# Streaming both parts of x past one loaded weight tile in a feed-forward up-projection

## The chip, the cores and the metric

The kernel runs on one core of a Trainium2 chip. The metric is device time in microseconds (us) of one execution of the whole program, the median of the runs shown. Engines are named as the profile names them: PE is the matrix engine (TensorE), PEld its weight loads, DVE the vector engine, ACT the scalar engine, POOL the GpSimd engine, SP the queue that issues the loads from memory.

## The reference

Two layers of a decoder on an input of 256 positions by 1024 features, in float32. Each layer is a mixer (three branches, merged and projected) and then a feed-forward block, each followed by a layer norm. The change touches only the feed-forward block:

```python
def _swiglu(x, w1, w3, w2):
    h = jax.nn.silu(jnp.einsum("bsd,df->bsf", x, w1)) * jnp.einsum("bsd,df->bsf", x, w3)
    return jnp.einsum("bsf,fd->bsd", h, w2).astype(x.dtype)
```

Here x is 256 x 1024, w1 and w3 are 1024 x 2816, w2 is 2816 x 1024. The two products with w1 and w3 are the up-projections; the one with w1 goes through silu and gates the other.

## The kernel before

**Numbers in two parts.** Matrix products run on numbers of type float32r, which keep fewer bits than float32. To keep accuracy, each float32 value is split into a high part (ACT copies it into float32r, `hi`) and a low part (DVE subtracts the high part from the value, `lo`). A product W x is then three products: W_hi x_hi + W_hi x_lo + W_lo x_hi. Each of the three is a matrix instruction of its own, with its own weight load, and all add into the same PSUM bank.

**The weights** stream from memory in units of 128 x 1024 floats (512 KB), one after the other in a fixed order, into four raw buffers. Each unit is split by one ACT and one DVE instruction (`split_w`, lines 416 to 438) into a `hi` and a `lo` tile. The split units are kept up to six ahead of PE (`AHEAD`, `fill`).

**The feed-forward block** of a layer has three stretches. The first 512 of the 2816 hidden columns are made token-major (tile `tm`, 512 columns of weights stream past x). The other 2304 hidden columns are made feature-major, 128 at a time: for f from 4 to 21, one unit of w1 and one of w3 (tile `f13`, shown as `f` in the profile). Then comes the down-projection with w2 (tile `w`), 22 units, into four banks (in the last layer five).

**One f in the kernel before** (lines 1274 to 1280): a PSUM bank of 512 columns is taken; w1's product fills its left 256 columns (the 256 positions), w3's its right 256. For each product `fm_acc` (line 458) runs over eight slices k of the 1024 features, three matrix instructions of 256 columns each. The side chain `f_fm` (line 1124) then reads the bank: ACT takes silu of the left half into `sg`, DVE multiplies the right half into `sg`, ACT and DVE split `sg` into the tiles `hh` (both parts are named so) that the down-projection uses.

**The order of the work.** All instructions of an engine run in the order in which they are emitted. That order comes from the class `Order` (line 159): it keeps an estimated clock for each engine, emits the main stream of matrix products, and emits the next step of a side chain once its estimate says that what the step needs is done. PSUM has eight banks, taken in turn; the small tiles such as `sg` have two buffers each.

**The parts of x** lie in four tiles of 1024 floats per partition (`xtile`, line 476), each with the high parts of two slices k in its first half and the low parts of the same two slices in its second.

Of the kernel before, what the change touches and what calls it, by code (L numbers as in the profile page):

```python
# [155 lines left out]


class Order:
    """Emission order: a main stream of matrix products and side chains whose next stage
    is emitted once the stage before it is expected to be done."""  # L160

    def __init__(self):
        self.clk = {e: 0.0 for e in ("pe", "act", "dve", "pool", "dma")}
# [86 lines left out]
def _build(ctx, nc, tc, ins, out):  # L250
# [87 lines left out]
    def rsqrt(o, i, e):  # L338
        G.tensor_tensor(out=o, in0=i, in1=e, op=ALU.pow)  # L339
        O.op("pool", 0.3 + 0.17 * n_of(o))  # L340
# [20 lines left out]
    def p2(t):  # L361
        return t.rearrange("p (t c) -> p t c", t=2)

    def pair2(name, dt=F32):
        return [p2(t) for t in pair(name, dt)]
# [4 lines left out]
    def rows(ap, n=P):  # L370
        return ap[:, None, :].to_broadcast([n, 4, P])

# [1 line left out]
    kc = const.tile([P, NK], F32, name="kc")  # L374
    xr = xres.tile([P, 2, D], F32, name="xr")
    ident = kc[:, K_ID:K_ID + P]
# [16 lines left out]
    sh8 = [P, 2, 4]  # L393
    mh8 = mhalf.rearrange("p (t h) -> p t h", t=2)

# [1 line left out]
    raws, ready, pos = [], [], [0, 0]  # L397

    def halves(i):
# [56 lines left out]
        return x[k // 2][:, k % 2]  # L456

    def fm_acc(o, w, x, c=slice(None)):
        """o[feature, token] = W^T x; w = (hi, lo) [128, k, columns], x = (hi, lo) tiles."""
        nk = w[0].shape[1]  # L460
        for k in range(nk):
            mm(o, w[0][:, k, c], xk(x[0], k), k == 0, False)
            mm(o, w[0][:, k, c], xk(x[1], k), False, False)
            mm(o, w[1][:, k, c], xk(x[0], k), False, k == nk - 1)

    def tm_acc(o, x, tk, w, k0, first, last):
        """o[token, column] += x^T W for the k-tiles of one unit from k-tile k0 on."""
        sl = slice(tk * P, (tk + 1) * P)
        nk = w[0].shape[1]
        for k in range(nk):  # L470
            xh, xl = (xk(x[q], k0 + k)[:, sl] for q in range(2))
            mm(o, xh, w[0][:, k], first and k == 0, False)
            mm(o, xl, w[0][:, k], False, False)
            mm(o, xh, w[1][:, k], False, last and k == nk - 1)

    def xtile(name):
        t = [pair2(name, F32R) for _ in range(4)]
        return [[a[q] for a in t] for q in range(2)]

    def log1p(o, t, tag, shape):  # L480
        """o = log(1 + t), t >= 0, compensated."""
        u, lg, e, d = (sm(tag + n, shape) for n in "uled")
        ts(u, t, 1.0, ADD)
        act_fn(lg, u, AF.Ln)
        ts(e, u, 1.0, ALU.is_equal)
        stt(d, u, -1.0, e, ADD, ADD)
        recip(d, d)
        tt(lg, lg, e, ADD)
        tt(lg, lg, t, MULT)
        tt(o, lg, d, MULT)  # L490

    def layer(l, xs, xtok):
# [5 lines left out]
        def done(n):  # L498
            O.done(k_(n))

# [1 line left out]
        def conv(dst, ps, w, ct, nct, bias):  # L502
            wv = lambda k, t: vc(w + nct * k + ct + t)
            for t in range(2):
# [51 lines left out]
            return  # L556
            yield

# [1 line left out]
        def b_scal():  # L560
            yield k_("smf")
            smf = B["smf"]
# [78 lines left out]
        def b_inv():  # L641
# [30 lines left out]
            B["bk"] = bk  # L672
            done("bk")
            yield
            # inverses of the diagonal 8x8 blocks by forward substitution: partition =
            # column of the inverse, each block's rows spread over its partitions
            at8 = AT.rearrange("p (t c) -> p t c", t=8)
            c32 = sub[:, 0:256].rearrange("p (t c) -> p t c", t=8)
            ac, z, tmp = (sub[:, 256 + 64 * n:320 + 64 * n].rearrange("p (t c) -> p t c", t=8)
# [143 lines left out]
            done("vb")  # L823

        def norm_gate(os, rs, gate, name, wo):
            """y = o rs rsqrt(mean((o rs)^2) + eps) w gate, to feature-major parts."""
            ss, f, m = (sm(name + n, sh8) for n in ("s", "f", "m"))
            sq = pair4("sq")
            for tk in range(2):
                act_fn(sq[tk], os[tk], AF.Square)  # L830
            yield
            for tk in range(2):
                rowsum(ss[:, tk], sq[tk])
            if rs is not None:
                tt(m, rs, rs, MULT)
                tt(ss, m, ss, MULT)
            ts(m, ss, 1.0 / P, MULT, 1e-6, ADD)
            yield
            rsqrt(f, m, mh8)
            if rs is not None:  # L840
                tt(f, f, rs, MULT)
            yield
            ys = pair4(name + "y")
            for tk in range(2):
                y = ys[tk]
                for h in range(4):
                    stt(y[:, h], os[tk][:, h], f[:, tk, h:h + 1], h4(B[gate, tk])[:, h],
                        MULT, MULT)
            yield
            hi, lo = [], []  # L850
            for t in range(2):
                ps = bank("pyf").rearrange("p (t k c) -> p t k c", t=2, k=2)
                for q in range(2):
                    for tk in range(2):
                        tp(ps[:, q, tk], ys[tk][:, 2 * t + q], ident)
                ps = ps.rearrange("p t k c -> p t (k c)")
                a, b = pair2(name + "h", F32R)
                act_fn(a, ps, AF.Copy, scale=vc(wo))
                stt(b, ps, vc(wo), a.bitcast(F32), MULT, SUB)
                hi.append(a), lo.append(b)  # L860
            B[name] = (hi, lo)
            done(name)

# [1 line left out]
        def c_copy(ps, nm):  # L865
            if nm == "cq":
                B["cqk"] = pair2(nm)
# [61 lines left out]
                co.append(o)  # L929
            yield from norm_gate(co, None, "sr", "yc", V_CN)  # L930

# [1 line left out]
        def a_gate(ps, j):  # L933
            ps = p2(ps)
            if j == 0:
# [60 lines left out]
            B["ya"] = yh, yl  # L996
            done("ya")

# [1 line left out]
        def g_chain(ps, b, j):  # L1000
            ps = p2(ps)
            if j % 2 == 0:
# [97 lines left out]
                r.append(t)  # L1100
            return r

# [1 line left out]
        hh = [None] * (NF // 2)  # L1104
        hl = [None] * (NF // 2)

# [5 lines left out]
        def f_tm(p3, tk):  # L1112
# [8 lines left out]
                split(*(x[:, :, tk * P:(tk + 1) * P] for x in h_tiles(q)), ps[:, 2 * q:2 * q + 2])  # L1121
            done(f"hT{tk}")

        def f_fm(ps, f):
            ps = p2(ps)
            sg = sml.tile([P, S], F32, tag="sg", name="sg")
            act_fn(sg, ps[:, 0], AF.Silu)
            yield
            tt(sg, ps[:, 1], sg, MULT)
            yield  # L1130
            hi, lo = h_tiles(f // 2)
            split(hi[:, f % 2], lo[:, f % 2], sg)
            done(f"h{f}")

# [1 line left out]
        def tm_group(x, chains, second):  # L1136
            """512-column token-major projections of four units each; with `second` the
            first token tile goes first, and the second once that token is there."""
            if second is None:
                for chain in chains:  # L1140
                    ps = [bank("tm") for _ in range(2)]
                    for q in range(4):
                        w = unit(2)
                        for tk in range(2):
                            tm_acc(ps[tk], x, tk, w, 2 * q, q == 0, q == 3)
                        if q == 3:
                            for tk in range(2):
                                O.spawn(chain(ps[tk], tk), 1)
                        yield
                return  # L1150
            u = []
            for tk in range(2):
                if tk:
                    yield second
                for n, chain in enumerate(chains):
                    ps = bank("tm")
                    for q in range(4):
                        if tk == 0:
                            u.append(unit(2, 1))
                        else:  # L1160
                            held[0] -= 1
                        tm_acc(ps, x, tk, u[4 * n + q], 2 * q, q == 0, q == 3)
                        if q == 3:
                            O.spawn(chain(ps, tk), 1)
                        if tk:
                            fill()
                        if q % 2:
                            yield
# [9 lines left out]
        def main():  # L1178
# [12 lines left out]
            O.spawn(small(pss), 0)  # L1191
            O.spawn(b_scal(), 2)
            yield
            mh, ml = xtile("mh")
            seen = []
            for u in MIX:
                nm, i = u[:-1], int(u[-1])
# [33 lines left out]
                    O.spawn(b_q(), 2)  # L1231
                if u == "v1":
                    O.spawn(b_v(), 2)
            # output projection
            if l == 0:
                nc.sync.dma_start(out=xr, in_=ins["xtm"])
            lv = ln_vecs(0)
# [19 lines left out]
            for tk in range(2):  # L1257
                for i in range(8 - tail, 8):
# [7 lines left out]
                    if i == 7:  # L1266
                        ahead[0] = 0
                    yield
            # feed-forward: hidden columns 0..511 token-major, the rest feature-major
            yield k_("x10")  # L1270

            yield from tm_group(x1, [lambda ps, tk: silu_tm(ps, "s1", tk), f_tm], k_("x11"))
            lv = ln_vecs(1)
            for f in range(4, NF):
                ps = bank("f13")
                for q in range(2):
                    fm_acc(p2(ps)[:, q], unit(8), x1)
                    if q:
                        O.spawn(f_fm(ps, f), 1)
                    yield  # L1280
            last = l + 1 == L
            x2 = None if last else xtile("x2")
# [40 lines left out]

        return main(), B, (k_("x20"), k_("x21"))

# [1 line left out]
    def everything():  # L1327
        xs, tok = xs0, ("xin", "xin")
        for l in range(L):
# [2 lines left out]
            xs, tok = B["x2"], t2_  # L1332

    with tc.manual_schedule(engines={mybir.EngineType.SP}):
        # the array's clock rises to its full rate only after some busy microseconds: let
        # it run while the first loads are under way
        warm = sml.tile([P, 512], BF16, tag="warm", name="warm")
        V.memset(warm, 0.0)
        pw = bank("warm")
# [108 lines left out]
```

## Time and profile before

| | us |
|---|---|
| median of 3 runs | 947.45 |
| lowest, highest | 945.55, 948.33 |
| span of the profiled execution | 945.9 |
| PE busy | 928.2 |
| DVE busy | 618.4 |
| ACT busy | 503.2 |

The profiled execution's own time is not given beside its span; the span runs from its first instruction to its last. Matrix instructions are pipelined: the duration shown for one reaches from its start to the modelled end of its passage, and overlaps the next one. How fast PE goes through a stream of them is therefore read from the distance between their starts, or from the length of a stretch and the number of instructions in it.

### The profile page before, as it was taken

What the parts mean: (1) busy time and instruction counts of PE and PEld (TensorE: products, weight loads), DVE (VectorE), ACT (ScalarE), POOL (GpSimd) and SP (SyncE); (2) the same over time, 40 slices, a digit from 0 to 9 for tenths busy, and PEclk for the clock granted to TensorE, in tenths of its full rate; (3) what the DMA queues carried; (4) which work ended last, traced back from release to release, by engine and by line L of the source; (5) the groups of instructions that cost most, each with busy time, mean ns of one, the idle gap of its engine ahead of it and who ended that gap; (6) DMA issues with size and microseconds to landing.
All of it is one profiled execution on the core that took longest, in us unless ns stands there. A gap on an engine that the chain in (4) does not pass through costs nothing.

```text
span 945.9 us, 16798 instructions
## 1 busy us (share of the span) xinstructions
PE 928.2 (98%) x6882; PEld 869.8 (92%) x6882; DVE 618.4 (65%) x893; ACT 503.2 (53%) x752; POOL 164.0 (17%) x81
## 2 busy tenths in 40 slices
PE   8999899999999999999999999999999999999996
PEld 5999799999988999998889999999999889999885
DVE  5587975595875655566457699586758646555715
ACT  5777569634633554455145775974547145444510
POOL 0445512630000000000033251254200000000001
PEclk9999999999999999999999999999999999999999
DMA  8854324546770855578325343254668247555801
GB/s 281 254 177 144 107 67 130 173 151 228 257 278 19 283 189 181 187 238 289 108 86 200 102 149 112 71 171 162 201 217 277 107 142 259 178 179 178 287 25 45
DMA packets 47997, 162.92 MB, mean 172 GB/s; under 512 B 7536, under 2 KB 8496, under 8 KB 47792
## 3 DMA queue, kind: packets, MB, share of 16 engines
q1 hardware_dynamic: 47776, 161.71, 51.2%
q8 instruction: 54, 0.88, 0.4%
q14 instruction: 23, 0.19, 0.1%
q10 hardware_dynamic: 144, 0.13, 0.0%
HBM read 160.77 MB, written 1.05 MB: 171 GB/s over the span
## 4 chain that ended last, share of the span: by engine, by line
PE 81%; DVE 9%; ACT 3%; DMA 3%; issue 2%; POOL 1%; SPq 0%; POOLq 0%; ACTq 0%; DVEq 0%
PE f L347 22%; PE fm L347 21%; PE w L347 13%; PE tm L347 8%; PE br L347 7%; PE wo L347 4%; DMA raw<-in_w_dram 3%; DVE lo L304 2%; ACT hi L292 1%; PE pt L347 1%; PE pp L347 1%; DVE sub L304 1%; DVE xa L315 1%; DVE q L315 1%; PE pr L347 1%
## 5 line engine op out<-in xcount | busy, mean ns | idle before, releaser
L304 DVE TENSOR_TENSOR lo<-raw,hi 128x1024 fp32r<-128x1024 f32 (+1 forms) x241 | 309.3, 1307 | 113.4 <-ACT hi L292 107.1
L292 ACT ACTIVATE hi<-raw 128x1024 fp32r<-128x1024 f32 (+1 forms) x293 | 299.3, 1052 | 92.3 <-DMA raw<-in_w_dram 83.0
L347 PE MATMUL fm<-x,hi 128*128 128x256 f32 x1536 | 283.7, 286 | 0.0
L347 PEld LDWEIGHTS fm<-x,hi 128*128 128x128 f32 x1536 | 240.0, 192 | 2.1 <-issue 1.5
L347 PE MATMUL fm<-x,lo 128*128 128x256 f32 x768 | 217.8, 284 | 0.0
L347 PE MATMUL f<-x,hi 128*128 128x256 f32 x1152 | 207.7, 283 | 0.0
L347 PEld LDWEIGHTS f<-x,hi 128*128 128x128 f32 x1152 | 179.8, 192 | 0.2
L432 POOL TENSOR_TENSOR lo<-raw,hi 128x1024 fp32r<-128x1024 f32 x52 | 136.0, 2617 | 231.0 <-ACT hi L292 227.4
L347 PE MATMUL f<-x,lo 128*128 128x256 f32 x576 | 163.0, 283 | 0.0
L347 PEld LDWEIGHTS fm<-x,lo 128*128 128x128 f32 x768 | 147.5, 192 | 0.0
L347 PE MATMUL w<-hi,hh 128*128 128x512 f32 (+1 forms) x396 | 111.2, 367 | 0.0
L347 PEld LDWEIGHTS f<-x,lo 128*128 128x128 f32 x576 | 110.6, 192 | 0.0
L347 PE MATMUL tm<-hi,x 128*128 128x512 f32 x320 | 100.8, 398 | 2.5 <-ACT hi L292 2.5
L339 POOL TENSOR_TENSOR rs<-rs,mhalf 128x1 f32<-128x1 f32 x8 | 7.5, 937 | 530.4 <-DVE rs L309 530.4
L347 PEld LDWEIGHTS w<-hi,hh 128*128 128x128 f32 x396 | 71.4, 189 | 12.2
L347 PEld LDWEIGHTS tm<-hi,x 128*128 128x128 f32 x320 | 59.2, 190 | 15.7 <-ACT hi L292 4.1
L347 PE MATMUL w<-lo,hh 128*128 128x512 f32 (+1 forms) x198 | 72.4, 365 | 0.0
L347 PE MATMUL tm<-lo,x 128*128 128x512 f32 x160 | 62.1, 391 | 0.1
L304 DVE TENSOR_TENSOR sg<-f,sg 128x256 f32<-128x256 f32 x36 | 15.1, 420 | 58.7 <-ACT sg L292 58.7
L292 ACT ACTIVATE sg<-f 128x256 f32<-128x256 f32 x36 | 13.8, 384 | 73.7 <-PE f L347 73.7
L347 PEld LDWEIGHTS w<-lo,hh 128*128 128x128 f32 x198 | 37.3, 188 | 6.1
L347 PE MATMUL wo<-hi,mh 128*128 128x512 f32 x128 | 40.0, 393 | 0.5 <-ACT mh L292 0.5
(273 smaller groups left out, 1092.0 us busy)
## 6 DMA issues: line engine op xcount, KB each, us to landing
raw<-in_w_dram SPq DMA_DIRECT2D x291, 512.0 KB, 4.6
lnv<-in_lnv_dram SPq DMA_DIRECT2D x8, 512.0 KB, 8.0
xr<-in_xtm_dram SPq DMA_DIRECT2D x1, 1024.0 KB, 8.3
xin<-in_xfm_dram SPq DMA_DIRECT2D x3, 256.0 KB, 7.3
raw<-in_w_dram SPq DMA_DIRECT2D x2, 256.0 KB, 3.5
ar<-in_aw_dram SPq DMA_DIRECT2D x8, 64.0 KB, 4.4
out_dram<-xr SPq DMA_DIRECT2D x2, 256.0 KB, 2.1
kc<-in_kc_dram SPq DMA_DIRECT2D x1, 476.0 KB, 8.8
```

Source lines behind the costliest of these rows:

```text
L292: ins_ = A.activation(o, i, f, **k)
L304: V.tensor_tensor(out=o, in0=a, in1=b, op=op)
L315: V.scalar_tensor_tensor(out=o, in0=a, scalar=s, in1=b, op0=op0, op1=op1)
L339: G.tensor_tensor(out=o, in0=i, in1=e, op=ALU.pow)
L347: T.matmul(o, w, x, start=start, stop=stop)
L432: G.tensor_tensor(out=lo, in0=t, in1=hi.bitcast(F32), op=SUB)
```

## The change

The eight slices of a unit take two matrix instructions each instead of three. The first streams 512 columns past the weight's high part: the 256 of x_hi and, from the other half of the same tile, the 256 of x_lo. They land in the left and the right half of one bank. The second streams x_hi past the weight's low part and adds to the left half. So a bank holds one unit's product only, in two halves that must be added when it is read: ACT copies the right half to SBUF, DVE adds the left half to it. w1's unit gets a side chain of its own (`f_gate`: copy, add, then silu), w3's another (`f_fm`: copy, add, multiply by the gate, split). `xtile` returns a third view of the same memory, in which the two parts of a slice stand beside each other. Only the feature-major up-projections of the feed-forward block change (18 f in each of two layers, two units each: 72 units); the mixer's feature-major projections still use `fm_acc`. Comments were removed too, and blank lines put in their place.

```diff
+    def fm_acc2(o, w, x):
+        nk = w[0].shape[1]
+        for k in range(nk):
+            mm(o, w[0][:, k], x[2][k // 2][:, k % 2], k == 0, False)
+            mm(o[:, 0], w[1][:, k], xk(x[0], k), False, k == nk - 1)
...
     def xtile(name):
-        t = [pair2(name, F32R) for _ in range(4)]
-        return [[a[q] for a in t] for q in range(2)]
+        v = [slot(name, F32R).rearrange("p (q k c) -> p k q c", q=2, k=2) for _ in range(4)]
+        return [t[:, :, 0] for t in v], [t[:, :, 1] for t in v], v
...
+        def f_gate(ps, f):
+            sg = sml.tile([P, S], F32, tag="sg", name="sg")
+            B["sg", f] = sg
+            cp(sg, ps[:, 1])
+            tt(sg, ps[:, 0], sg, ADD)
+            yield
+            act_fn(sg, sg, AF.Silu)
+            done(f"sg{f}")
+
         def f_fm(ps, f):
-            ps = p2(ps)
-            sg = sml.tile([P, S], F32, tag="sg", name="sg")
-            act_fn(sg, ps[:, 0], AF.Silu)
-            yield
-            tt(sg, ps[:, 1], sg, MULT)
+            sg = B["sg", f]
+            hv = sml.tile([P, S], F32, tag="hv", name="hv")
+            cp(hv, ps[:, 1])
+            tt(hv, ps[:, 0], hv, ADD)
+            yield k_(f"sg{f}")
+            tt(sg, hv, sg, MULT)
             yield
             hi, lo = h_tiles(f // 2)
             split(hi[:, f % 2], lo[:, f % 2], sg)
...
             for f in range(4, NF):
-                ps = bank("f13")
-                for q in range(2):
-                    fm_acc(p2(ps)[:, q], unit(8), x1)
-                    if q:
-                        O.spawn(f_fm(ps, f), 1)
+                for chain in (f_gate, f_fm):
+                    ps = p2(bank("f13"))
+                    fm_acc2(ps, unit(8), x1)
+                    O.spawn(chain(ps, f), 1)
                     yield
```

The order of the instructions on PE at the start of the feature-major stretch of the first layer (tile `f_3502` is the bank, `x_3157` the tile of x, `hi` and `lo` the parts of the weight unit; "x2" means two in a row; `-` is before, `+` after):

```order
 L347 MATMUL tm<-hi,x_3160 128x512 x2
 L347 MATMUL tm<-lo,x_3160 128x512
-L347 MATMUL f_3502<-x_3157,hi 128x256 x2
+L347 MATMUL f_3502<-x_3157,hi 128x512
 L347 MATMUL f_3502<-x_3157,lo 128x256
```

Two products of 256 columns with the same weight became one of 512; this repeats for every slice, and apart from it and from the bank that w3's unit writes, PE's order is the same in the whole program.

The order on ACT in the middle of that stretch, over two f, in the kernel before (`sg` is the gate, `hh` the split hidden column, `hi<-raw` the split of a weight unit):

```order
L292 ACTIVATE sg_4064<-f13_3966 128x256
L292 ACTIVATE hh_4000<-sg_4064 128x256
L292 ACTIVATE sg_4130<-f13_4033 128x256
L292 ACTIVATE hh_4133<-sg_4130 128x256
L292 ACTIVATE hi_4136<-raw_4007 128x1024
L292 ACTIVATE hi_4167<-raw_4038 128x1024
L292 ACTIVATE hi_4202<-raw_4073 128x1024
L292 ACTIVATE hi_4233<-raw_4104 128x1024
```

and in the changed kernel, also over two f (`hv` is the copy of the right half of w3's bank; `sg<-f13` is now the copy, and `sg<-sg` the silu):

```order
L292 ACTIVATE sg_3835<-f13_3781 128x256
L292 ACTIVATE hi_3895<-raw_3786 128x1024
L292 ACTIVATE hi_3923<-raw_3813 128x1024
L292 ACTIVATE sg_3835<-sg_3835 128x256
L292 ACTIVATE hv_3862<-f13_3808 128x256
L292 ACTIVATE sg_3891<-f13_3838 128x256
L292 ACTIVATE hh_3832<-sg_3835 128x256
L292 ACTIVATE sg_3891<-sg_3891 128x256
L292 ACTIVATE hv_3918<-f13_3865 128x256
L292 ACTIVATE hh_3945<-sg_3891 128x256
L292 ACTIVATE hi_3953<-raw_3843 128x1024
L292 ACTIVATE hi_3979<-raw_3870 128x1024
```

Each f has two more ACT instructions, and the splits of the weights come two at a time instead of four.

## Rows read from the trace of the kernel before

**Rows 1.** The page, part 1: busy time, share of the span, instructions.
```profile
PE 928.2 (98%) x6882; PEld 869.8 (92%) x6882; DVE 618.4 (65%) x893; ACT 503.2 (53%) x752; POOL 164.0 (17%) x81
```

**Rows 2.** Chain that ended last, in order of time: start us, us, what.
```profile
309.64 5.75 PE f L347 x48
315.83 97.92 PE f L347 x816
413.75 55.79 PE w L347 x246
...
772.73 5.75 PE f L347 x48
778.92 97.92 PE f L347 x816
876.84 61.07 PE w L347 x330
```

**Rows 3.** Busy time by stretch, both feature-major stretches: engines' busy us, PEclk, DMA share, GB/s.
```profile
309.60:413.75 104.15, 104.15 (x870) 104.15 (x869) 60.09 (x76) 51.53 (x75) 0.00 (x0) 1.00 0.61 205
772.70:876.80 104.10, 104.10 (x870) 104.10 (x869) 60.13 (x76) 51.53 (x76) 0.00 (x0) 1.00 0.61 204
```

**Rows 4.** PE in order of time, 256-column products: start us, us, engine, line, what.
```profile
340.03 0.28 PE L347 MATMUL f<-x,lo 128*128 128x256 f32 x1
340.15 0.40 PE L347 MATMUL f<-x,hi 128*128 128x256 f32 x2
340.39 0.28 PE L347 MATMUL f<-x,lo 128*128 128x256 f32 x1
```

**Rows 5.** PE in order of time, 512-column products of the down-projection.
```profile
429.71 0.39 PE L347 MATMUL w<-lo,hh 128*128 128x512 f32 x1
429.93 0.62 PE L347 MATMUL w<-hi,hh 128*128 128x512 f32 x2
430.39 0.39 PE L347 MATMUL w<-lo,hh 128*128 128x512 f32 x1
430.61 0.62 PE L347 MATMUL w<-hi,hh 128*128 128x512 f32 x2
431.07 0.39 PE L347 MATMUL w<-lo,hh 128*128 128x512 f32 x1
```

**Rows 6.** Page, part 5: up-projections by form, busy us, mean ns | idle before.
```profile
L347 PE MATMUL f<-x,hi 128*128 128x256 f32 x1152 | 207.7, 283 | 0.0
L347 PE MATMUL f<-x,lo 128*128 128x256 f32 x576 | 163.0, 283 | 0.0
```

**Rows 7.** One tile (sg, then hh): count, duration ns min/median/max, starts, forms.
```profile
L292 ACT ACTIVATE sg<-f x36: 367/385/385, 315.4 to 876.9; 128x256 f32<-128x256 f32 x36
L304 DVE TENSOR_TENSOR sg<-f,sg x36: 414/418/425, 315.9 to 878.0; 128x256 f32<-128x256 f32 x36
L292 ACT ACTIVATE hh<-sg x36: 397/418/421, 320.6 to 879.4; 128x256 fp32r<-128x256 f32 x36
L304 DVE TENSOR_TENSOR hh<-sg,hh x36: 416/426/428, 322.1 to 880.6; 128x256 fp32r<-128x256 f32 x36
```

**Rows 8.** ACT and DVE in order of time: four weight splits in a row.
```profile
340.17 3.89 ACT L292 ACTIVATE hi<-raw 128x1024 fp32r<-128x1024 f32 x4
...
341.24 4.63 DVE L304 TENSOR_TENSOR lo<-raw,hi 128x1024 fp32r<-128x1024 f32 x4 [0.52 <-ACT hi L292]
```

**Rows 9.** Waits: engine line waited for: total us, times, longest us.
```profile
ACT sg L292 <- PE f L347: 73.7, 35, 4.2
DVE sg L304 <- ACT sg L292: 58.7, 17, 3.8
```

More of the change, by code (lines that the diff above doesn't have):

```diff
@@ L1193, in main @@
             yield
-            mh, ml = xtile("mh")
+            mh, ml, _ = xtile("mh")
             seen = []
```

## Prediction

> **What bounds the kernel now.** I read the busy shares first. PE is busy 98% of the span and no other engine over two thirds except the weight loads, which run beside PE [rows 1]. That share alone proves nothing, since overlapping durations count as busy without a gap, so I went on to the chain that ended last, in order of time. The reader is to see there that each feature-major stretch of the feed-forward block is two pieces, 48 and 816 products, with PE as the only engine: 864 products, 18 f times two units times 24, with four short transposes between the pieces [rows 2]. So in these stretches the end is set by how fast PE issues products, and the third view, the busy times by stretch, says what stands beside it: ACT 51.5 and DVE 60.1 us of 104.15, the DMA at 0.61, the clock granted in full (1.00, the level of 2.4 GHz) [rows 3]. The waits agree: ACT's gate step waited 73.7 us in all for PE [rows 9], while the up-projections had no idle time before them [rows 6]. The changed edits lie entirely in these two stretches.
>
> **The pace of PE.** The listed 283 ns of a product [rows 6] is its passage and not its pace. The pace comes from starts and lengths:
> - 256 columns: 97.92 us for 816 products, 120.0 ns each [rows 2]; the starts say the same, 340.03 to 340.39 for three [rows 4].
> - 512 columns: 429.71 to 430.39 and to 431.07, 0.68 us for three each time, 226.7 ns each [rows 5].
>
> The difference, 106.7 ns for 256 columns, is 0.417 ns per column. What is left over is 120.0 - 106.7 = 13.3 ns per product, whatever its length. Do the two paces add up when lengths are mixed? The last layer's down-projection has 22 units of nine products of 512 and six of 256: 22 x (9 x 226.7 + 6 x 120.0) = 60.7 us, against 61.07 measured for its 330 products [rows 2]. They do, within 0.6%.
>
> The Trainium skill (TensorE: Matmul & The Clock Gate, section "Wait — 56ns, not 53.3ns?") gives a warm matmul a fixed cost of about 2.5 ns beyond its columns. By that, 576 products saved would be an estimated 1.4 us. The trace differs: 13.3 ns here, in both lengths, and the measurement decides.
>
> **The change part by part.**
> 1. *Removed on PE.* A unit takes 24 x 120.0 = 2.880 us now. Afterwards it has eight products of 512 and eight of 256: 8 x (226.7 + 120.0) = 2.773 us. The columns are the same, 6144; eight fixed parts of 13.3 ns go, 0.107 us per unit. There are 18 f x 2 units x 2 layers = 72 units: 576 products and 576 weight loads fewer, 72 x 0.107 = **7.7 us**, all of it on the chain.
> 2. *The streamed operand in two runs.* The 512 columns are two runs of 256 that lie half a tile apart. The trace has no product whose streamed operand is broken in two. From the one side: it costs as a 512-column product of one run, 226.7 ns [rows 5]. From the other: as two products, 240.0 ns [rows 4], and then all 7.7 us are gone. Below 226.7 I see no reason, since the columns alone are 213.3 ns and the second product of each slice keeps its fixed part. I take 226.7: it is one instruction with one weight load, as in rows 5, and the fixed part comes once per instruction in every row.
> 3. *Added on ACT.* Per f two more instructions of 128 x 256: the copies out of PSUM, priced as the silu read out of PSUM, 0.385 us [rows 7]. The silu itself stays and reads SBUF; I leave its price. 72 instructions, 28 us of work. Per two f ACT goes from 51.53/9 = 5.73 to 7.27 us.
> 4. *Added on DVE.* Per f two adds with one operand in PSUM, 0.418 us as the product that reads PSUM now; that product afterwards reads SBUF only, as the split of `hh` does, 0.426 us, the same within 2% [rows 7]. 72 instructions, 30 us. Per two f DVE goes from 60.09/9 = 6.68 to 8.35 us.
> 5. *What hides 3 and 4.* Two f last 4 x 2.773 = 11.09 us on PE. ACT would fill 66% of it and DVE 75%. Both queues are in order: behind a copy that waits for PE stand weight splits, and behind those PE's later weights. But units are split up to six ahead, some 16 us of PE work, and the longest wait of ACT for PE is 4.2 us [rows 9]. In the order over two f, silu stands behind two weight splits, some 1.9 us (half of 3.89 for four [rows 8]), which cover the add of 0.418 that it waits for; only the second f's silu and split are exposed to DVE directly. The banks, one per unit now and eight in turn, come round after eight units, 22 us, against a read-out of two instructions. I cost all this at nothing; without that cover it is the slower rival below.
> 6. *The loads.* Two units per f, in 5.55 instead of 5.76 us: 205 GB/s become 213, with the DMA at 0.61 of its time [rows 3]. Nothing.
> 7. *The end of a stretch.* After the last product, copy, add, product and split make 0.385 + 0.418 + 0.418 + 0.418 + 0.426 = 2.1 us, one copy-and-add more than now. The down-projection needs this f in its last unit, over 50 us later [rows 2]. Nothing.
>
> **The sum.** Against the profiled span: 945.9 - 7.7 = 938.2 us. The median of the runs is 947.45, so 1.55 us lie around the span or between executions; with them the forecast is **939.8 us**, 0.8% faster.
>
> **The rivals.**
> - *The two runs are paid as two* (chance 0.07). No row has such an operand, which is what speaks for it. Against it speaks that the fixed part is the same at 256 and at 512 columns, so it goes with the instruction. Time: 8 x (240 + 120) = 2.880 us per unit, 947.5 us, no change. The same sign, at 946, would follow if only a small piece of the 13.3 ns went with the instruction (0.02).
> - *PE's pace is met, but not everywhere* (0.05): at the start of a stretch the first weights come late, because ACT waits for the first unit's product sooner and the splits behind it move back. Of the first eight units in each layer ACT is then the pace; half of the gain is lost, 943.6 us.
> - *Slower: the hand-offs between ACT and DVE become the pace* (0.04). Place: the two queues in the middle of the stretches, where copy, add, silu, copy, add, product and split alternate between the engines and the weight splits stand in the same queues. If they never overlapped, two f would take 7.27 + 8.35 = 15.6 us against 11.52 now, 18 times over, 74 us; six units of lead, 17 us in each layer, take away 33 of it: some 988 us. It decides from the point at which either queue needs more than 11.09 us for two f; DVE would have to lose 2.7 us there to waiting. For it speaks DVE's 75%; against it that ACT and DVE now keep waiting for PE and for each other without holding it up [rows 3, 9].
>
> **How the numbers follow.** What a measurement can tell from no change is 0.3%, 2.8 us; faster means below 944.6. The forecast has 0.82, and it lies with its neighbours between 937 and 942. Faster: 0.82 and most of the second rival, 0.86. Same: the first rival and the rest, 0.10. Slower: 0.04. The range of 8 in 10 runs from 937.0 to 944.5 us: it takes in the half gain, and leaves out most of the first rival and all of the slower one.
>
> **What would show it.** Step 1: the chain still has the feature-major stretches as PE alone, with about 100.3 us in place of 104.15, and 6306 products and weight loads instead of 6882. Step 2: starts in a unit alternate by 227 and 120 ns; 240 and 120 would make the first rival right. Steps 3 to 5: ACT some 65 us and DVE some 75 us busy per stretch, and no idle time on PE or on its weight loads that ends with `hi` or `lo`; any such wait shows the second rival or the slower one. The rest of the program should keep its times, shifted by 3.8 us from the first layer's down-projection on. A time above 944.6 or a stretch over 102 us would make the prediction wrong.

## The result, and the profile after

| | before, us | after, us | ratio of after to before, 95% interval |
|---|---|---|---|
| first comparison | 947.88 | 941.51 | 0.9946 (0.9931 to 0.9961) |
| second, another chip run | 947.14 | 942.55 | 0.9951 (0.9934 to 0.9969) |
| third | 946.41 | 942.07 | 0.9949 (0.9932 to 0.9966) |

The change makes the kernel faster by about 0.5%, some 5 us. The forecast was 939.8 us, 7.7 us less than before, with a range from 937.0 to 944.5. The direction and the place are right; the gain that was forecast is too large.

The page of the profile after, first its busy times (us, share of the span, instructions):

```profile
PE 922.5 (98%) x6306; PEld 838.3 (89%) x6306; DVE 644.5 (69%) x965; ACT 523.6 (56%) x824; POOL 162.4 (17%) x81
```

Against [rows 1] there are 576 products and 576 weight loads fewer, and 72 instructions more on DVE and on ACT each, as the prediction counted them. The chain that ended last, in order of time (start us, us, what), where it answers to [rows 2]:

```profile
308.18 5.65 PE f L347 x32
314.26 96.10 PE f L347 x544
410.36 55.82 PE w L347 x246
...
768.70 5.64 PE f L347 x32
774.78 94.29 PE f L347 x544
869.08 61.07 PE w L347 x330
```

Still PE alone. But the two stretches differ: 544 products are 34 units, so a unit took 96.10/34 = 2.826 us in the first layer and 94.29/34 = 2.773 in the second. The second is the forecast's value to the nanosecond. The first gives back half of the 0.107 us that a unit should save. The two units ahead of each long piece took 5.65 and 5.64 us, 2.82 each, so in the second layer too they were slow; its faster pace begins behind the four short transposes between the pieces.

The profiled spans differ by 945.9 - 938.0 = 7.9 us, close to the forecast, but by accident: the two stretches (from the first product of `f` to the first of `w`) became 1.9 and 3.7 us shorter, 5.7 in all, and of the rest 1.5 us come from ahead of the first stretch (308.18 against 309.64), which the change does not touch. The busy times by stretch, which answer to [rows 3]:

```profile
308.18:410.36 102.18, 102.18 (x581) 88.64 (x581) 73.25 (x112) 62.54 (x111) 0.00 (x0) 1.00 0.62 211
768.70:869.08 100.38, 100.38 (x582) 87.76 (x581) 73.15 (x112) 62.70 (x111) 0.00 (x0) 1.00 0.63 215
```

The columns of times are the length of the stretch, PE, PEld, DVE and ACT. The reader is to see that DVE and ACT are equally busy in both, within 0.2 us, and that the clock is granted in full in both (1.00, the level of 2.4 GHz). So where are the 1.8 us? In the starts of PE's products. In the first layer (start us, us, engine, line, what):

```profile
339.89 0.40 PE L347 MATMUL f<-x,hi 128*128 128x512 f32 x1
340.12 0.28 PE L347 MATMUL f<-x,lo 128*128 128x256 f32 x1
340.24 0.40 PE L347 MATMUL f<-x,hi 128*128 128x512 f32 x1
340.48 0.28 PE L347 MATMUL f<-x,lo 128*128 128x256 f32 x1
340.60 0.40 PE L347 MATMUL f<-x,hi 128*128 128x512 f32 x1
340.84 0.28 PE L347 MATMUL f<-x,lo 128*128 128x256 f32 x1
340.95 0.40 PE L347 MATMUL f<-x,hi 128*128 128x512 f32 x1
```

and in the second layer:

```profile
802.36 0.39 PE L347 MATMUL f<-x,hi 128*128 128x512 f32 x1
802.59 0.27 PE L347 MATMUL f<-x,lo 128*128 128x256 f32 x1
802.70 0.40 PE L347 MATMUL f<-x,hi 128*128 128x512 f32 x1
802.93 0.28 PE L347 MATMUL f<-x,lo 128*128 128x256 f32 x1
803.05 0.39 PE L347 MATMUL f<-x,hi 128*128 128x512 f32 x1
803.28 0.27 PE L347 MATMUL f<-x,lo 128*128 128x256 f32 x1
803.39 0.40 PE L347 MATMUL f<-x,hi 128*128 128x512 f32 x1
```

Count three pairs in each: 340.95 - 339.89 = 1.06 us, 353 ns per pair, and 803.39 - 802.36 = 1.03 us, 343 ns per pair. The pattern repeats through the whole long piece (in the unrounded starts of the trace 361, 349, 350 ns from pair to pair in the one, 343, 350 in the other), and the 272 pairs of the piece give the means: 96.10/272 = 353.3 ns and 94.29/272 = 346.7. The same instructions run in one of two rhythms, called slow and fast below.

The waits that answer to [rows 9] (engine, line waited for, total us, times, longest us):

```profile
DVE hv L304 <- ACT hv L292: 29.6, 16, 2.4
ACT sg L292 <- PE f L347: 27.6, 17, 2.2
ACT hv L292 <- PE f L347: 21.3, 17, 1.5
...
DVE sg L304 <- ACT sg L292: 5.0, 13, 0.5
```

ACT's two reads of a bank still wait for PE, 27.6 + 21.3 = 48.9 us where it was 73.7, and PE itself has no wait before a product of `f`. So the read-out holds up nothing in these stretches.

### The profile page after: what moved, and what is told of

Read it like the earlier page. It is cut to its first block, busy times and chain, and to the rows that moved or that the text cites. A ratio compares the mean times of both kernels' runs of the same rounds, so it can differ in the third digit from the quotient of the medians.

```text
span 938.0 us, 15814 instructions
## 1 busy us (share of the span) xinstructions
PE 922.5 (98%) x6306; PEld 838.3 (89%) x6306; DVE 644.5 (69%) x965; ACT 523.6 (56%) x824; POOL 162.4 (17%) x81
## 4 chain that ended last, share of the span: by engine, by line
PE 92%; DVE 5%; DMA 1%; issue 1%; ACT 1%; POOL 0%; SPq 0%; POOLq 0%
PE fm L347 26%; PE f L347 22%; PE w L347 13%; PE tm L347 11%; PE br L347 7%; PE wo L347 5%; PE pt L347 1%; PE pp L347 1%; DVE sub L304 1%; DMA raw<-in_w_dram 1%; DVE lo L304 1%; PE pr L347 1%; PE px L355 1%; PE pln L355 1%; DVE xa L315 1%
## 5 line engine op out<-in xcount | busy, mean ns | idle before, releaser
L347 PE MATMUL f<-x,hi 128*128 128x512 f32 x576 | 202.0, 396 | 0.0
L347 PE MATMUL f<-x,lo 128*128 128x256 f32 x576 | 160.7, 279 | 0.0
L347 PEld LDWEIGHTS f<-x,hi 128*128 128x128 f32 x576 | 108.1, 188 | 26.1
L347 PEld LDWEIGHTS f<-x,lo 128*128 128x128 f32 x576 | 108.5, 188 | 0.1
L292 ACT ACTIVATE x<-pln 128x256 fp32r<-128x256 f32 x24 | 7.9, 383 | 60.7 <-PE pln L355 60.7
L292 ACT ACTIVATE gt<-fm,vecs 128x256 f32<-128x256 f32 x48 | 20.3, 468 | 33.7 <-PE fm L347 33.6
```

Of the source, the lines that this page charges most:

```text
L292: ins_ = A.activation(o, i, f, **k)
L347: T.matmul(o, w, x, start=start, stop=stop)
```

## The experiments

Each kernel is the changed one with the edit shown. The ratio is that to the kernel before the change, with its 95% interval.

**The same kernel again.** No edit.

> The changed kernel once more, unchanged. In its first profile the pair of products (512 then 256 columns) took 353.3 ns on average in the first layer's stretch (starts 361, 349, 350 ns apart, over and over) and 346.7 in the second layer's (343, 350). If this is a rhythm into which the pair falls by the moment at which it starts, the two means may change places or both be one of the two in this profile: 544 products in 94.3 or in 96.1 us. If it comes from the layer's addresses, the first layer has 96.1 and the second 94.3 again. Time 941.5 either way, within 1.5 us.

Measured 942.55 us, ratio 0.9951 (0.9934 to 0.9969). The chain in order of time:

```profile
315.29 96.10 PE f L347 x544
...
776.02 96.10 PE f L347 x544
```

Both layers are in the slow rhythm now, with the same program. So the layer alone, with its addresses, does not decide the rhythm. Nor does the execution alone: that of the first profile had both, and within its second layer the rhythm changed at the transposes.

**Three products instead of two**, everything else kept:

```diff
-            mm(o, w[0][:, k], x[2][k // 2][:, k % 2], k == 0, False)
+            mm(o[:, 0], w[0][:, k], xk(x[0], k), k == 0, False)
+            mm(o[:, 1], w[0][:, k], xk(x[1], k), False, False)
             mm(o[:, 0], w[1][:, k], xk(x[0], k), False, k == nk - 1)
```

> The changed kernel with its 512-column product written as two of 256 (left half, right half), with a weight load each; banks, read-out and order as in the changed kernel. If the gain is the fixed 13.3 ns of each product, all of it goes: 24 starts 120 ns apart in a unit, 97.9 us for 816 products, time as before the change, 947.9 us (ratio to before 1.000). If the gain comes from anything else in the change (a bank per unit, the separate side chains, the splits two at a time), it stays near 941.5.

Measured 947.5 us, ratio 0.9998 (0.9983 to 1.0013). Its chain:

```profile
315.18 97.92 PE f L347 x816
...
778.84 97.92 PE f L347 x816
```

Exactly the 97.92 us of [rows 2]. Banks, side chains and the order of the splits are worth nothing by themselves in these stretches and cost nothing there: the whole gain is in the merged product.

**One run instead of two.** In `xtile` the parts of a slice are put next to each other:

```diff
-        v = [slot(name, F32R).rearrange("p (q k c) -> p k q c", q=2, k=2) for _ in range(4)]
+        v = [slot(name, F32R).rearrange("p (k q c) -> p k q c", q=2, k=2) for _ in range(4)]
```

> The changed kernel with the parts of a slice of x next to each other, so that the 512 streamed columns are one run. If the two runs cost the 6.6 ns that a pair of products took too long in the first layer, both stretches show 346.7 ns per pair, 94.3 us for 544 products, and the time falls by 1.8 us to 939.7. If the alternation of 512 and 256 columns does, the starts show the same two rhythms (343/350 or 361/349/350) as in the changed kernel, and the time stays at 941.5 within 1.5 us.

Measured 942.34 us, ratio 0.9946 (0.9930 to 0.9962):

```profile
314.49 96.10 PE f L347 x544
...
775.40 96.10 PE f L347 x544
```

The slow rhythm in both layers, without any break in the operand. The break is not needed for it.

**Equal lengths together.** A unit's eight products of 512 columns first, then its eight of 256; the operand in two runs as in the changed kernel:

```diff
         for k in range(nk):
             mm(o, w[0][:, k], x[2][k // 2][:, k % 2], k == 0, False)
+        for k in range(nk):
             mm(o[:, 0], w[1][:, k], xk(x[0], k), False, k == nk - 1)
```

> The changed kernel with a unit's eight products of 512 columns first and its eight of 256 after them; the operand is still in two runs. If the alternation makes the slow rhythm, starts are 226.7 ns apart in the eight and 120 in the other eight, 2.773 us per unit in both layers (94.3 us for 544 products), and the time falls by 1.8 us, to 939.7. If the two runs do, the eight products of 512 columns stay some 6 ns too far apart in the first layer, 233 ns, and the time stays at 941.5.

Measured 939.14 us, ratio 0.9915 (0.9895 to 0.9935), below the changed kernel's 942.55 of the same runs (938.64 to 939.92 against 940.72 to 944.18, no overlap). Its chain, and one unit in order of time:

```profile
314.82 94.98 PE f L347 x544
...
774.18 94.98 PE f L347 x544
```

```profile
339.80 2.00 PE L347 MATMUL f<-x,hi 128*128 128x512 f32 x8
341.64 1.11 PE L347 MATMUL f<-x,lo 128*128 128x256 f32 x8
342.60 0.63 PE L347 MATMUL f<-x,hi 128*128 128x512 f32 x2
```

Both layers alike. The eight of 512 took 341.64 - 339.80 = 1.84 us, 230 ns each, and the eight of 256 took 0.96, 120 each. So it is the alternation that makes the slow rhythm. Grouping also keeps the weight's two parts and the halves of the bank from alternating, but in the kernel with three products both alternate at equal length, and there every start is 120 ns after the last; the lengths are what is left. The expected 2.773 us per unit was not reached: 94.98/34 = 2.7935, 20 ns per unit still lost. In the unrounded starts of the trace the first five products of 512 take 233, 236, 228, 232 and 231 ns, 28 ns too long together, the others 227; the first two of 256 take 113 and 119, 8 ns too short, the others 120.

**How the loss goes with the number of changes.** Two groups of four in a unit, and sixteen with both units of an f together:

```diff
-        for k in range(nk):
-            mm(o, w[0][:, k], x[2][k // 2][:, k % 2], k == 0, False)
-        for k in range(nk):
-            mm(o[:, 0], w[1][:, k], xk(x[0], k), False, k == nk - 1)
+        for k0 in range(0, nk, 4):
+            for k in range(k0, k0 + 4):
+                mm(o, w[0][:, k], x[2][k // 2][:, k % 2], k == 0, False)
+            for k in range(k0, k0 + 4):
+                mm(o[:, 0], w[1][:, k], xk(x[0], k), False, k == nk - 1)
```

> As the kernel with grouped products (eight of 512 columns, then eight of 256 in a unit), but in two groups of four: two changes of length there and back per unit instead of one, against eight in the changed kernel. Grouped, a unit took 2.7935 us, 20 ns more than 8 x (226.7 + 120.0). If each change there and back costs those 20 ns, a unit takes 2.813 us now, 95.7 us for 544 products, and the time is 1.4 us above the grouped one's, 940.5. If the loss is a rhythm that only strict alternation falls into, it stays at 95.0 us and 939.1.

```diff
-                for chain in (f_gate, f_fm):
-                    ps = p2(bank("f13"))
-                    fm_acc2(ps, unit(8), x1)
-                    O.spawn(chain(ps, f), 1)
+                ps = [p2(bank("f13")) for _ in range(2)]
+                w = []
+                for q in range(2):
+                    w.append(unit(8))
+                    for k in range(8):
+                        mm(ps[q], w[q][0][:, k], x1[2][k // 2][:, k % 2], k == 0, False)
+                    yield
+                for q, chain in enumerate((f_gate, f_fm)):
+                    for k in range(8):
+                        mm(ps[q][:, 0], w[q][1][:, k], xk(x1[0], k), False, k == 7)
+                    O.spawn(chain(ps[q], f), 1)
                     yield
```

> Both units of an f together: sixteen products of 512 columns into two banks, then sixteen of 256. Half the changes of length of the grouped kernel. If each change there and back costs 20 ns, a unit takes 2.783 us, 94.6 us for 544 products, and the time falls by 0.7 us to 938.4. If the read-out, which now comes for both units at once, holds something up, the time rises and PE shows idle time in the stretch.

Measured 940.13 us, ratio 0.9930 (0.9915 to 0.9945), and 938.68, ratio 0.9913 (0.9898 to 0.9928). Their chains, first the groups of four, then the sixteen:

```profile
314.59 95.21 PE f L347 x544
```

```profile
314.27 95.59 PE f L347 x552
```

In groups of four a unit took 95.21/34 = 2.800 us, 27 ns over the sum of the two paces. With sixteen the 552 products are 272 of 512 and 280 of 256, by the two paces 95.26 us; 0.33 us over that for some 17 f is 10 ns per unit, as expected. Both layers are alike in both kernels. So per unit, counting a change there and back as one: half a change 10 ns, one 20, two 27, eight 53 in the slow rhythm and none in the fast. A fixed price per change, 20 ns, holds only for groups of eight and sixteen; at two changes 40 ns were expected and 27 came. Of the runs here the sixteen together have the lowest median, but the interval overlaps that of the grouped kernel (0.9895 to 0.9935).

**The read-out left out**, on the grouped kernel; the product of the weight's high part with the low part of x is then missing from the result:

```diff
-            cp(sg, ps[:, 1])
-            tt(sg, ps[:, 0], sg, ADD)
-            yield
-            act_fn(sg, sg, AF.Silu)
+            act_fn(sg, ps[:, 0], AF.Silu)
...
-            cp(hv, ps[:, 1])
-            tt(hv, ps[:, 0], hv, ADD)
...
-            tt(sg, hv, sg, MULT)
+            tt(sg, ps[:, 0], sg, MULT)
```

> The grouped kernel without the added read-out: silu and the product read the left half of the bank alone, so the right half (the weight's high part times the low part of x) is left out of the result; 72 ACT copies and 72 DVE adds fewer. If PE hides the read-out, the stretches keep 95.0 us for 544 products and the time stays at 939.1. If the added work of ACT and DVE held up PE, or the weights of a later stage, the time falls by more than 1 us.

Measured 939.72 us, ratio 0.9922 (0.9908 to 0.9937); the chain's pieces are 94.98 us again in both layers. DVE fell to 60.7 us in the first layer's stretch and ACT to 51.7:

```profile
308.60:409.70 101.10, 101.10 (x582) 89.05 (x581) 60.68 (x77) 51.66 (x76) 0.00 (x0) 1.00 0.62 211
```

With the read-out the first layer's stretch has 73.3 and 62.7 us in the grouped kernel. PE hides the read-out completely.

**The same for the mixer's gates.** A first kernel, on the grouped one, in which some gates were taken from the wrong tile (the instructions are the same, the values not):

> The grouped kernel with the same treatment for the merge gates of the mixer (24 units per layer, sigmoid after copy and add). By the grouped kernel's pace a unit saves 2.880 - 2.7935 = 0.0865 us, 48 units 4.2 us: 935.0 us. The rival: in the mixer ACT and DVE also carry the chains of the three branches, and 48 more copies and adds delay what PE waits for there; then PE shows more idle time between 140 and 265 us and the time stays at 939 or rises.

Measured 940.03 us, ratio 0.9932 (0.9916 to 0.9948). The 4.2 us did not come, and PE has a wait of 1.7 us in the mixer that the grouped kernel has not. Then with the right tiles, on the kernel with sixteen together:

```diff
-        def g_chain(ps, b, j):
+        def g_chain(ps, b, j, t, gt):
...
-            for t in range(2):
-                act_fn(gt[:, t], ps[:, t], AF.Sigmoid, bias=vc(V_GB + 8 * b + 2 * j + t))
+            cp(gt[:, t], ps[:, 1])
+            tt(gt[:, t], ps[:, 0], gt[:, t], ADD)
+            yield
+            act_fn(gt[:, t], gt[:, t], AF.Sigmoid, bias=vc(V_GB + 8 * b + 2 * j + t))
```

> The kernel with both units of an f together, and in addition the merge gates of the mixer by the new form (24 units per layer, a bank, a copy, an add and a sigmoid per unit; eight products of 512 columns, then eight of 256). If PE hides the read-out there too, 48 units save 0.0865 us each against the 938.7 us of the kernel with both units together: 934.5. If ACT and DVE, which carry the three branches beside the gates, come late with what PE needs next, PE shows idle time between 140 and 265 us and between 590 and 768 us, and the time stays within 1.5 us of 938.7 or rises.

Measured 943.14 us, ratio 0.9955 (0.9940 to 0.9971), worse than the 938.68 (0.9898 to 0.9928) it started from, by the ratios some 4 us. The profile, of its fastest execution, shows 1.8 of them (a span of 939.3 us against 937.5). PE's waits now have one of 3.0 us for ACT in the delta-rule branch, and in the stretch with it PE is idle for 2.2 us and the mean clock granted 0.98:

```profile
PE po L347 <- ACT w L292: 3.0, 1, 3.0
```

```profile
180.00:266.00 86.00, 83.80 (x565) 78.24 (x566) 71.02 (x87) 54.18 (x80) 15.51 (x6) 0.98 0.63 212
```

DVE is at 71 of 86 us there, with the branch chains in the same queue; with sixteen together and the old gates it was at 64, and PE was not idle. Right behind the wait, from 182.5 to 185.8 us, the granted clock is 0.50, its lower level of 1.2 GHz. In the second layer the chain that ended last leaves PE for 38 us ahead of the mixer's output projection `wo` and runs over the gates' steps (`gt`), weight splits and loads, where with sixteen together it stayed on PE:

```profile
688.74 2.81 PE fm L347 x16
...
691.63 0.39 ACT gt L292
...
729.77 11.63 PE wo L347 x50
```

A gate's unit did become shorter, 2.81 us (2.88 before). What was free in the feed-forward block is not free here. That the added copies and adds are what delays the branch's step on ACT is argued from these queues; no run took them apart.

**The rhythm once more.**

> The changed kernel unchanged, for its rhythm in a third execution. So far three stretches of four had 96.1 us for 544 products and one had 94.3, with the same program. If the moment of the start decides, either value may come in either layer, and nothing between or above; if something of the first chip decided, both layers have 96.1 again. Time between 940 and 943.5.

Measured 942.07 us, ratio 0.9949 (0.9932 to 0.9966), 96.10 us in both layers. Over four profiles of alternating products (three of the changed kernel, one with the operand in one run) seven stretches of eight were slow behind the transposes, and all eight ahead of them. Six of the seven come from one chip; that of the first profile is not on record, so whether the chip has a part in it stays open.

## Why the prediction was right, and where its size was off

- *What bounds it, and step 1's mechanism*: right. PE's pace sets the two stretches, and 576 products fewer is the whole gain; with the third product back, the gain is gone (ratio 0.9998, 0.9983 to 1.0013).
- *Step 1's size*: mis-sized, and this is why the forecast was too good. It took a pair for 226.7 + 120.0 = 346.7 ns. It measured 353.3 in seven of eight stretches. A unit then saves 54 ns and not 107: over 72 units 3.9 us and not 7.7, and 5.7 in the profile with one fast stretch. The three medians lie 6.4, 4.6 and 4.3 us below those of before.
- *Step 2*, the operand in two runs: right. In one run nothing changed, so the two runs cost nothing that these runs can tell. But the sign named for it, starts that alternate by 227 and 120 ns, did not come in either rhythm: the unrounded starts alternate by 236 and 117 ns on average in the slow one and by 232 and 115 in the fast.
- *Steps 3 to 5*, the read-out: right. Some 65 us on ACT and 75 on DVE per stretch were forecast, 62.5 and 73.2 measured; left out, it gives back no time on PE.
- *Steps 6 and 7*: right. The DMA was busy for 0.62 and 0.63 of the stretches, and the down-projection follows without a gap.
- *The rivals and the range*: the half gain, 943.6 us, is near what was measured, but not by its mechanism: no weight came late in these stretches. (Nor does its story give a half: the first eight units of each layer are 16 of 72, 1.7 us of the 7.7.) The range reached to 944.5 to take in that rival, so it is in part luck that 941.5 to 942.5 lie in it. The slower rival, the hand-offs between ACT and DVE, is off in the feed-forward block; a delay that fits it appears in the mixer, where 24 more units per layer of the same form cost some 4 us.
- *The signs of being wrong*: the prediction named a time above 944.6 or a stretch over 102 us. The time stayed below. The first layer's stretch took 102.18 us, and both layers' in the two later profiles of the same kernel about as much, so by its own second sign the sum of step 1 was wrong there.
- *The 13.3 ns against the 2.5 ns of the Trainium skill* (TensorE: Matmul & The Clock Gate, section "Wait — 56ns, not 53.3ns?"): the estimate of 1.4 us from that figure was too small; all three comparisons exclude it.

**The hint in the trace of before.** The prediction held 60.7 us, worked out for the mixed products of the last down-projection, against 61.07 measured [rows 2], and called that agreement within 0.6%. But there a unit of nine products of 512 and six of 256 comes round after 879.45 - 876.67 = 2.78 us, where its two paces add up to 2.76:

```profile
876.67 0.63 PE L347 MATMUL w<-hi,hh 128*128 128x512 f32 x2
...
879.45 0.63 PE L347 MATMUL w<-hi,hh 128*128 128x512 f32 x2
```

That is 20 ns per unit with one change of length there and back, the same 20 as in groups of eight, and the change was about to bring eight changes into each unit, for a gain of 107 ns. The hint gave no better number: eight times 20 ns would have made a slower kernel, and 53 or nothing came. It said that the term was not known to within its own size. The check should have been held against the term, not against the total. And "13.3 ns whatever its length" could not fail: a line through two paces always leaves the same rest at both. Each product fewer gave 13.3 ns in the fast rhythm alone and 6.7 in the slow one.

What stays open is why a change of length costs time, and what sets one rhythm or the other when the products start again behind the transposes. That alternation does it is shown by grouping; the mechanism inside PE was not tried, since no view here shows it.

## What to carry to other kernels

On a stream that PE alone bounds, fewer and longer products save a fixed part each: at most 13.3 ns here, of which strict alternation mostly left 6.7, groups of eight 10.8 and groups of sixteen 12.1. It is worth paying for that with work on engines that wait, as long as the chain stays on PE; in the mixer it did not. Put products of equal length together: grouping by length was worth 2.4 us by the two stretches (100.98 us each instead of 102.18) and 3.4 by the medians, for one more line. Hold a check of a pace against the size of the gain that rests on it, not against the total.

## What the runs showed of the hardware that was not expected

Products of 512 and of 256 columns in strict alternation run in one of two rhythms, 353.3 or 346.7 ns per pair, with the same program falling into either (96.10 and 94.29 us for 544 products); the one change of rhythm seen within a stretch came at four short transposes. In groups of eight the first five products of 512 are late and the first two of 256 early, 20 ns late in all per change there and back; groups of sixteen lose the same 20 ns, groups of four 13.3, and strict alternation 6.7 or nothing. And 512 columns streamed from two places half a tile apart go as fast as from one (96.10 us for 544 products in both).
